# The down projection of a SwiGLU feed-forward in seven block products, with the weight differences made during the input projection

## The chip, the cores and the metric

One NeuronCore of a Trainium2 chip runs the whole program; the other seven are idle. The metric is the device time of one execution in microseconds. Engine names are those of the profile: PE multiplies matrices, DVE, ACT and POOL work element by element, SP issues transfers.

## The reference, cut to what matters

One decoder layer over 2048 prompt rows and 8 x 4 sample rows, d_model 1024, feed-forward width 2816. The part that changes is the last product of the feed-forward:

```python
def _swiglu(x, g, w_gate, w_up, w_down):
    h = _rmsnorm(x, g)
    return (jax.nn.silu(h @ w_gate) * (h @ w_up)) @ w_down

x = x + jnp.concatenate([att, u * gate], axis=-1) @ w_out
x = x + _swiglu(x, norm2_g, w_gate, w_up, w_down)      # then a last RMSNorm
```

The outputs are float32, and the products are made on PE from operands that are split into a high and a low part, as (high, high), (high, low) and (low, high): each product of two blocks is three matmuls.

## The kernel before, in words

The program runs in three stretches: the input projection (its last matmul starts at 565 us; the sample rows' attention stands between its products), the prompt's attention (to about 884 us), and then output projection and feed-forward in three blocks of token tiles of 128 rows: tiles 0-5, 6-11, and 12-15 with the sample rows. All matmuls stand on PE in an order written by hand; a clock of steps (`tick`, `later`, and in the input projection `Plan.at`) puts the other engines' work between them. Each engine, SP included, takes its instructions in the order in which they were written.

In a block the feed-forward goes over 22 chunks of 128 hidden columns. For a chunk f, `product` makes seven block products q = 0..6 of gate and up projection together (lines L1607 to L1609, twelve matmuls of 384 columns each, 272 in the last block). That part is already a scheme of seven products in place of eight. Its seven weight operands per chunk are made from sources that lie in `ab_d` (block 0 makes them and stores them; the others load them), by `high` on ACT (L1546) and `low_half` on POOL (L1550). Each product's result goes to one of four PSUM banks (`ps_m`) and is added up by DVE (L1619 to L1636); `hidden` multiplies silu(gate) by up (L1653), splits the result into `hw`, high on ACT (L1657) and low on DVE (the row of L1275 or L1642).

The down projection is plain. Every two chunks, at q = 3, 4 and 5 of an even chunk, `down_unit` takes one token tile after the other: for each half of the 1024 output columns six matmuls of 512 columns (two chunks by three parts, L1680) go to one of two banks `ps_o`, and DVE adds the bank to the tile's accumulator `acc` (L1682). Two weight rows of 128 x 1024 (`load_down`, one buffer `fd`) are split by ACT (L135) and POOL (L138) for it.

Between two blocks, `next_block` runs the last pair's down products (`first_downs`, L1696 and L1698, then `down_unit`), and in the same time splits the next block's inputs (`split_cat`, L1365 on ACT and L1366 on DVE) and output weights (`split_wo`), finishes the old tiles (`final_a`, `final_b` L1716, `final_store` L1722) and loads the new ones (`load_acc` L1303). Then come the output projection's first half for all tiles (`open_unit`), its second half (`second_unit`), and the norm.

In the input projection POOL has the products of the sample rows' keys (L536), the gate's layer norm (L383) and low halves (L138); PE waits for the low halves `vnl` in the gate products at L412.

## Time and profile before

| what | value |
|---|---|
| runs | 2497.45, 2494.05, 2496.11 us; median 2496.11 us |
| profiled execution | span 2494.2 us, 39114 instructions; the page gives no other time for it, and the span lies 1.9 us under the median of the runs |
| PE, weight load, DVE, ACT, POOL busy | 98%, 85%, 51%, 45%, 52% of the span |
| granted PE clock, mean | 0.990 |
| down matmuls (L1680 and L1696) | 2112 of 128 rows and 88 of 64 rows, all 512 columns wide |
| bytes moved | 455.36 MB, mean 183 GB/s |

Busy times are unions over an engine's instructions. Matmuls overlap in the records, so the mean length of one is not the distance from one to the next; that distance is read from a run of them.

### The profile page before, as it was taken

Reading aid. Unit: us, or ns where it says so; the run is one execution under the profiler, and the core shown is the slowest. Engines: PE = TensorE matmul, PEld = TensorE weight load, DVE = VectorE, ACT = ScalarE, POOL = GpSimd, SP = SyncE. Lnnn points to the kernel's source line nnn. Section 1 sums busy time; section 2 is a strip of 40 time slices with the busy share of each in tenths; the row PEclk is TensorE's granted clock in tenths of the full one; section 3 lists DMA queues with packets and bytes.
Section 4 is the critical chain, followed back from the end, with each engine's and each line's share of the span. In section 5 each row is a group of like instructions: output and inputs, shape, how many; then the busy total and the mean of one; then the engine's idle time right before and its main releaser. Section 6 shows DMA issues by size and latency. Waiting matters only on the chain.

```text
span 2494.2 us, 39114 instructions
## 1 busy us (share of the span) xinstructions
PE 2434.1 (98%) x14022; PEld 2114.0 (85%) x14022; DVE 1265.1 (51%) x2595; ACT 1131.2 (45%) x2449; POOL 1300.3 (52%) x1019
## 2 busy tenths in 40 slices
PE   9999999999999999999999999999999999999997
PEld 7877776667888678999999988999999987999997
DVE  4557573216767644444444465444444466444445
ACT  6324343226667556555455356323323345444334
POOL 2216441004777636777677544544545534676665
PEclk9999999999999899999999999999999999999999
DMA  9874835685555463646556372553544554665553
GB/s 297 274 232 150 271 110 160 201 268 184 173 177 160 117 215 114 195 152 193 167 160 195 126 228 101 192 189 132 196 179 151 203 163 140 224 210 187 189 194 136
DMA packets 292292, 455.36 MB, mean 183 GB/s; under 512 B 28711, under 2 KB 160984, under 8 KB 286980
## 3 DMA queue, kind: packets, MB, share of 16 engines
q1 hardware_dynamic: 285252, 440.82, 54.1%
q10 hardware_dynamic: 6848, 12.06, 1.7%
q8 instruction: 111, 1.82, 0.3%
q14 instruction: 81, 0.66, 0.1%
HBM read 365.07 MB, written 157.84 MB: 210 GB/s over the span
## 4 chain that ended last, share of the span: by engine, by line
PE 73%; DVE 2%; POOL 2%; ACT 2%; issue 1%; DMA 1%; SPq 0%; DVEq 0%; ACTq 0%; POOLq 0%
PE ps_o L1680 19%; PE ps_m L1609 11%; PE ps_m L1607 11%; PE ps_m L1608 11%; PE ps_s L856 2%; PE ps_o L911 2%; PE ps_t L883 1%; PE ps_s L935 1%; PE ps_s L318 1%; PE ps_o L1374 1%; PE ps_o L1376 1%; PE ps_o L1375 1%; PE ps_m L1374 1%; PE ps_s L320 1%; PE ps_s L319 1%
## 5 line engine op out<-in xcount | busy, mean ns | idle before, releaser
L1550 POOL TENSOR_TENSOR op<-fr,op 128x512 fp32r<-128x512 f32 x385 | 487.3, 1296 | 259.3 <-ACT op L1546 245.2
L1607 PE MATMUL ps_m<-xh,op 128*128 128x384 f32 (+3 forms) x1904 | 604.9, 318 | 0.9 <-ACT xh L1451 0.5
L1609 PE MATMUL ps_m<-xh,op 128*128 128x384 f32 (+3 forms) x1904 | 604.6, 318 | 0.0
L1608 PE MATMUL ps_m<-xl,op 128*128 128x384 f32 (+3 forms) x1904 | 603.9, 317 | 0.1
L1680 PE MATMUL ps_o<-dw,hw 128*128 128x512 f32 x2040 | 480.5, 391 | 4.0 <-DVE acc L1682 3.3
L1680 PEld LDWEIGHTS ps_o<-dw,hw 128*128 128x128 f32 x2040 | 380.4, 188 | 82.5 <-DVE acc L1682 5.1
L1607 PEld LDWEIGHTS ps_m<-xh,op 128*128 128x128 f32 x1904 | 360.4, 189 | 5.3 <-ACT xh L1451 0.7
L1608 PEld LDWEIGHTS ps_m<-xl,op 128*128 128x128 f32 x1904 | 360.0, 189 | 4.0 <-DVE xl L1463 0.4
L1682 DVE TENSOR_TENSOR acc<-acc,ps_o 128x512 f32<-128x512 f32 (+1 forms) x362 | 248.1, 687 | 224.8 <-PE ps_o L1680 224.8
L1609 PEld LDWEIGHTS ps_m<-xh,op 128*128 128x128 f32 x1904 | 359.9, 189 | 0.0
L1647 ACT ACTIVATE ps_t<-zn 128x384 f32<-128x384 f32 (+1 forms) x126 | 58.3, 463 | 469.3 <-DVE zn L1630 381.5
L1546 ACT ACTIVATE op<-fr 128x512 fp32r<-128x512 f32 x396 | 235.4, 624 | 25.6 <-DMA fr<-ab_d 21.0
L138 POOL TENSOR_TENSOR dw<-fd,dw 128x1024 fp32r<-128x1024 f32 x66 | 158.6, 2403 | 162.9 <-ACT dw L135 162.9
L318 PE MATMUL ps_s<-wh,xh 128*128 128x512 f32 x480 | 197.5, 411 | 6.1 <-ACT xh L135 6.1
L320 PE MATMUL ps_s<-wh,xl 128*128 128x512 f32 x480 | 189.6, 395 | 0.0
L319 PE MATMUL ps_s<-wl,xh 128*128 128x512 f32 x480 | 189.5, 395 | 0.0
L1550 POOL TENSOR_TENSOR op<-pair,op 128x512 fp32r<-128x512 f32 x63 | 81.3, 1298 | 113.6 <-ACT op L1546 109.2
L536 POOL TENSOR_TENSOR pr<-kv,qb 96x512 f32<-96x512 f32 x32 | 44.3, 1383 | 172.4 <-DMA kv<-in_cache_k_dram 90.8
L318 PEld LDWEIGHTS ps_s<-wh,xh 128*128 128x128 f32 x480 | 91.5, 191 | 48.8 <-issue 23.7
L1657 ACT ACTIVATE hw<-ps_t 128x384 fp32r<-128x384 f32 (+1 forms) x126 | 54.7, 450 | 162.0 <-DVE ps_t L1653 162.0
L927 POOL CAST sq<-k 128x512 fp32r<-128x512 f32 x32 | 34.0, 1063 | 164.1 <-PE ps_s L319 164.1
L1518 ACT ACTIVATE fr<-fr,g2c 128x128 f32<-128x128 f32 x352 | 108.3, 388 | 0.0
(490 smaller groups left out, 4277.0 us busy)
## 6 DMA issues: line engine op xcount, KB each, us to landing
fr<-ab_d SPq DMA_DIRECT2D x308, 256.0 KB
fd<-in_w_down_dram SPq DMA_DIRECT2D x66, 512.0 KB
out_ks_dram<-in_cache_k_dram SPq DMA_DIRECT2D x56, 512.0 KB
out_vs_dram<-in_cache_v_dram SPq DMA_DIRECT2D x56, 512.0 KB
ab_d<-fr SPq DMA_DIRECT2D x88, 256.0 KB
qk_d<-pair SPq DMA_DIRECT2D x64, 256.0 KB
ab_d<-pair SPq DMA_DIRECT2D x63, 256.0 KB
kv<-in_cache_k_dram SPq DMA_DIRECT2D x64, 192.0 KB
```

Of the source, the lines that this page charges most:

```text
L138: (eng_lo or pool).tensor_sub(lo, src, hi.bitcast(F32))
L318: pe.matmul(o[j], xh[:, k, :], wh, start=(k == 0), stop=False)
L319: pe.matmul(o[j], xh[:, k, :], wl, start=False, stop=False)
L320: pe.matmul(o[j], xl[:, k, :], wh, start=False, stop=(k == KD - 1))
L1518: act.activation(w_[:, k * P:(k + 1) * P], w_[:, k * P:(k + 1) * P], AF.Copy, scale=g2c[:, kk:kk + 1])
L1546: act.activation(ops[f, j][0], ab[f][j], AF.Copy)
L1550: (pool if f or j in POOL_LOW else dve).tensor_sub(lo_, ab[f][j], hi.bitcast(F32))
L1607: pe.matmul(out, wh[:, ks], xh[:, :, k], start=(k == 0), stop=False)
L1608: pe.matmul(out, wh[:, ks], xl[:, :, k], start=False, stop=False)
L1609: pe.matmul(out, wl[:, ks], xh[:, :, k], start=False, stop=(k == 3))
L1680: pe.matmul(ps[0:nr], l_, r_[:, cs], start=(z == 0 and y == 0), stop=(z == FC - 1 and y == len(pairs) - 1))
L1682: dve.tensor_add(B.acc[i][0:nr, cs], B.acc[i][0:nr, cs], ps[0:nr])
```

## The change: what it does

The down projection's operands are cut in a 2 x 2 scheme: the two rows of blocks are the two token tiles of a pair, the shared dimension is the two chunks of a pair (f = 2n, 2n + 1), the columns are the two halves of the 1024. Seven block products replace the eight, with sums and differences on both sides (`TO` says to which accumulator each is added, `FRESH` which ones start a bank anew; the others go on adding in the same bank after DVE has read it).

- Weights: `down_rows`, `down_sums` and `down_keep` run at steps 80 to 210 of the input projection. For each of 11 pairs they load two 128 x 1024 rows, make four sums of 128 x 512 on POOL and store the seven 128 x 512 sources in a new array `dd_d`. In the feed-forward `load_dw` fetches one source per product into one of two places, issued right after the product that used the place before; `split_dw`, two steps ahead of the product, splits it by ACT and by POOL (odd products of the first and last block: DVE).
- Hidden values: an even chunk's values are kept in `h0`; `h_even` and `h_odd` make four sums per pair on DVE and split seven operands (`hop`) by ACT and DVE, in place of four splits.
- Products: `down_product` runs one of the seven every second step, for all pairs of tiles; each one's results are added to `acc` by DVE right away. The gate and up products keep three banks in place of four.
- Between blocks, `next_block` runs the product left over from the pair before and the last pair's seven, with `h_odd` between them. The old tiles are finished from step 9 on, one per step (before: from step 2 on, every second step); the new tiles' first additions come 4 steps later, their half-1 weights 2 steps later.
- The very last pair of the last block stays plain (`plain_down`).

On DVE between block 0 and block 1 (`acc`: accumulators, `ps_o`, `ps_m`: banks of the down products, `ps_t`, `h`: hidden values, `zn`, `raw`: sums, `hop`, `hw`: operands, `xl`: the next block's inputs), before:

```order
L1653 TENSOR_TENSOR ps_t0_14560<-ps_t0_14560,raw_14541 128x384
L1642 TENSOR_TENSOR hw_14646<-ps_t1_14621,hw_14646 128x6x64
L1642 TENSOR_TENSOR hw_14646<-ps_t0_14560,hw_14646 128x6x64
L1698 TENSOR_TENSOR acc0_9112<-acc0_9112,ps_o2_14670 128x512
L1698 TENSOR_TENSOR acc0_9112<-acc0_9112,ps_m2_14671 128x512
L1698 TENSOR_TENSOR acc1_9110<-acc1_9110,ps_o3_14672 128x512
L1698 TENSOR_TENSOR acc1_9110<-acc1_9110,ps_m3_14673 128x512
L1366 TENSOR_TENSOR xl2_14658<-xl2_14658,xh2_14657 128x1024
```

and in the changed kernel:

```order
L1797 TENSOR_TENSOR ps_t0_14976<-ps_t0_14976,raw_14941 128x384
L1645 TENSOR_TENSOR op_15063<-op_15063 128x512
L1712 TENSOR_TENSOR zn_15117<-h0_9266,ps_t0_14976 128x3x64
L1712 TENSOR_TENSOR zn_15117<-h0_9266,ps_t1_15057 128x3x64
L1713 TENSOR_TENSOR zn_15118<-zn_15117,h0_9266 128x384
L1662 TENSOR_TENSOR acc0_9289<-acc0_9289,ps_o2_15067 128x512
L1662 TENSOR_TENSOR acc2_9543<-acc2_9543,ps_o3_15072 128x512
L1662 TENSOR_TENSOR acc4_9639<-acc4_9639,ps_m3_15077 128x512
L1682 TENSOR_TENSOR hop_10053<-zn_15118,hop_10053 128x384
L1721 TENSOR_TENSOR raw_15144<-ps_t0_14976,zn_15118 128x3x64
L1682 TENSOR_TENSOR hop_10054<-ps_t0_14976,hop_10054 128x3x64
L1721 TENSOR_TENSOR raw_15144<-ps_t1_15057,zn_15118 128x3x64
```

Two operand rows and then one addition for every six matmuls have become sums and splits that stand between the additions, and one addition for every three matmuls: 24 of them up to the first row of the output projection, where there were 12.

On POOL in the first half's gate columns (`vnl`, `zn`: the gate's low halves and layer norm, `pr`: key products), before:

```order
L138 TENSOR_TENSOR vnl<-zn,vnh 128x512
L536 TENSOR_TENSOR pr<-kv,qb 96x512
L536 TENSOR_TENSOR pr<-kn,qb 128x512
L383 TENSOR_TENSOR zn<-zn,lnb 128x512
L138 TENSOR_TENSOR vnl<-zn,vnh 128x512
L383 TENSOR_TENSOR zn<-zn,lnb 128x512
L536 TENSOR_TENSOR pr<-kv,qb 96x512
```

and in the changed kernel (`tw`, `tu`: rows and sums of the down weights):

```order
L385 TENSOR_TENSOR zn<-zn,lnb 128x512
L140 TENSOR_TENSOR vnl<-zn,vnh 128x512
L632 TENSOR_TENSOR tu<-tw 128x512
L629 TENSOR_TENSOR tw<-tw 128x512
L385 TENSOR_TENSOR zn<-zn,lnb 128x512
L632 TENSOR_TENSOR tu<-tw 128x512
L632 TENSOR_TENSOR tu<-tw,tu 128x512
L538 TENSOR_TENSOR pr<-kv,qb 96x512
```

The four sums of a pair stand between two layer-norm rows and ahead of the key products.

The diff, cut to its core:

```diff
@@ ps_m
-            turn[3] = which = (turn[3] + 1) % 4
+            turn[3] = which = (turn[3] + 1) % 3
@@ new: weight sums
+    def down_rows(n):
+        for z in range(2):
+            dn[n, z] = w_ = sp.tile([P, 2, DA], F32, name="tw", tag="tw", bufs=2)
+            f = 2 * n + z
+            sync.dma_start(w_, A["w_down"][f * P:(f + 1) * P, :].rearrange("p (a c) -> p a c", a=2))
+    def down_sums(n, j):
+        (b11, b12), (b21, b22) = ((dn[n, z][:, 0], dn[n, z][:, 1]) for z in range(2))
+        if j == 1:
+            pool.tensor_sub(b12, b12, b11)
+            return
+        dn[n, "t", j] = t_ = sp.tile([P, DA], F32, name="tu", tag="tu", bufs=3)
+        pool.tensor_sub(t_, *((b22, b12) if j == 3 else (b22, b12) if j == 2 else (b21, dn[n, "t", 2])))
@@ plan of the input projection
+    for n, s0 in enumerate([80, 89, 98] + [134 + 10 * i for i in range(NF // 2 - 3)]):
+        at(s0, "misc", down_rows, n)
+        for j, x in ((3, 3), (1, 3), (2, 4), (4, 4)):
+            at(s0 + x, "out", down_sums, n, j)
+        for j, x in ((3, 5), (0, 5), (2, 6), (4, 6), (1, 6)):
+            at(s0 + x, "store", down_keep, n, j)
@@ new: products
+    PLACE = (0, 4, 5, 6, 2, 1, 3)
+    TO = ((0, 0), (0, 1), (1, 1), (1, 0), (0, 0), (1, 1), (0, 1))
+    FRESH = (0, 4, 5)
+    SLOT = (2, 4, 6, 8, 10, 12, 14)
+    def load_dw(B, k, place=None):
+        n, p = divmod(k, 7)
+        B.dw[k] = x = place or B.ring[k % 2]
+        sync.dma_start(x[1].bitcast(F32), dd_d[n, :, PLACE[p]])
+    def split_dw(B, k):
+        hi, lo_ = B.dw[k]
+        act.activation(hi, lo_.bitcast(F32), AF.Copy)
+        (dve if k % 2 and (B.last or B.b0 == 0) else pool).tensor_sub(lo_, lo_.bitcast(F32), hi.bitcast(F32))
+    def down_product(B, k):
+        n, p = divmod(k, 7)
+        ...
+        for j in range(B.nt // 2):
+            if new:
+                B.chain[j] = bank(2 + j) if j < 2 else ps_m(3)
+            ps, ts = B.chain[j], slice(j * P, (j + 1) * P)
+            for y, (l_, r_) in enumerate(((hh[:, ts], dh), (hh[:, ts], dl), (hl[:, ts], dh))):
+                pe.matmul(ps, l_, r_, start=(new and y == 0), stop=(y == 2), skip_group_check=True)
+            x = B.acc[2 * j + odd]
+            dve.tensor_add(x[:, cs], x[:, cs], ps)
+        ...
@@ new: operands of an odd chunk (a11, a21 from h0; a12, a22 from this chunk)
+    def h_odd(B, u, part):
+        ...
+        if part == 0:
+            ...
+            for z in range(2):
+                dve.tensor_add(u["s1"][:, :, z], a21[:, :, z], a22[z])
+            dve.tensor_sub(u["s2"], u["s1"], a11)
+            high_of(B, 1, u["s2"], 0, n)
+            for z in range(2):
+                high_of(B, 3, a22[z], 0, n, z)
+        elif part == 1:
+            lows_of(B, 1, u["s2"], 0, n)
+            u["s4"] = op_view(raw_tile()[:, 0:n * P], 0, n)
+            for z in range(2):
+                dve.tensor_sub(u["s4"][:, :, z], a12[z], u["s2"][:, :, z])
+                lows_of(B, 3, a22[z], 0, n, z)
+                high_of(B, 4, a12[z], 0, n, z)
+            high_of(B, 5, u["s1"], 0, n)
+        else:
+            for z in range(2):
+                lows_of(B, 4, a12[z], 0, n, z)
+            high_of(B, 6, u["s4"], 0, n)
+            lows_of(B, 5, u["s1"], 0, n)
+            lows_of(B, 6, u["s4"], 0, n)
@@ hidden
-        dve.tensor_mul(g, g, c)
-        ...
-        act.activation(hi, g[:, :, 0:64], AF.Copy)
-        lows = [(lo_, g[:, :, 0:64], hi.bitcast(F32))]
+        if f % 2:
+            dve.tensor_mul(g, g, c)
+            ...
+        else:
+            h = B.h0[:, :, a // 2:b // 2, zz].rearrange("p o j w -> p j o w")
+            dve.tensor_mul(h, *(x.rearrange("p (j o w) -> p j o w", o=2, w=B.w) for x in (g, c)))
@@ next_block
-            later(2 + 2 * y, fn)
+            later(9 + y, fn)
         for y, i in enumerate(order):
-            later(12 + 2 * y, first_end, B, i)
+            later(16 + 2 * y, first_end, B, i)
-        for fn in downs:
-            fn()
+        K = 7 * (NF // 2 - 1)
+        for y in range(-1, 7):
+            if 0 <= y + 1 < 3:
+                h_odd(prev, prev.u, y + 1)
+            if y == -1:
+                split_dw(prev, K + 6)
+            down_product(prev, K + y)
+            split_wo(B, 0, y + 1, lambda s: op_tile())
+            tick()
@@ steps of a block
+            for n in (f // 2 - 2, f // 2 - 1, f // 2):
+                for p in range(7):
+                    k, t_ = 7 * n + p, 14 * (n + 1) + SLOT[p]
+                    ...
+                    if x == t_ - 2:
+                        split_dw(B, k)
+                    if x == t_:
+                        down_product(B, k)
+                    t_ = 14 * ((k - 2) // 7 + 1) + SLOT[(k - 2) % 7] if k > 1 else 9 + k
+                    if x == t_:
+                        load_dw(B, k)
```

More of the change, by code (lines that the diff above doesn't have):

```diff
@@ new lines, in load_dw @@
+    def load_dw(B, k, place=None):
[8 more added lines that the diff above has]
+        n, p = divmod(k, 7)
+        dh, dl = B.dw.pop(k)
+        hh, hl = B.hop[p]
+        odd, half = TO[p]
+        cs = slice(half * 512, (half + 1) * 512)
+        new = p in FRESH
+        for j in range(B.nt // 2):
[6 more added lines that the diff above has]
+            dve.tensor_add(x[:, cs], x[:, cs], ps)
+        if B.last and p in (0, 4, 5, 6):
+            if p < 6:
+                B.chain["s"] = ps_m(3)
+            ps = B.chain["s"][0:2 * SR]
+            hs_ = hs4[:, n % 2 * 2 + (p in (4, 6))]
+            for y, r_ in enumerate((dh, dl)):
+                pe.matmul(ps, hs_, r_, start=(p < 6 and y == 0), stop=(y == 1), skip_group_check=True)
+            x = B.acc[B.nt]
+            for half in ((0, 1), (0,), (), (1,))[(0, 4, 5, 6).index(p)]:
+                cs = slice(half * 512, (half + 1) * 512)
+                dve.tensor_add(x[0:2 * SR, cs], x[0:2 * SR, cs], ps)
@@ new lines, in op_view, with lows_of, high_of, h_even @@
+    def op_view(x, a, b):
+        return x.rearrange("p (j z c) -> p j z c", z=2, c=64)[:, a:b]
+    def lows_of(B, p, src, a, b, z=None):
+        hi, lo_ = (op_view(x, a, b) for x in B.hop[p])
+        if z is not None:
+            hi, lo_ = hi[:, :, z], lo_[:, :, z]
+        dve.tensor_sub(lo_, src, hi.bitcast(F32))
+    def high_of(B, p, src, a, b, z=None):
+        hi = op_view(B.hop[p][0], a, b)
+        act.activation(hi if z is None else hi[:, :, z], src, AF.Copy)
+    def h_even(B, u):
+        a, b = u["a"] // 2, u["b"] // 2
+        a11, a21 = (B.h0[:, o, a:b, :, 0:64] for o in range(2))
+        plain = B.last and u["f"] + 2 == NF
+        high_of(B, 0, a11, a, b)
+        if plain:
+            s3 = a21
+        else:
+            s3 = op_view(zn_tile()[:, 0:(b - a) * P], 0, b - a)
+            dve.tensor_sub(s3, a11, a21)
+        high_of(B, 2, s3, a, b)
+        lows_of(B, 0, a11, a, b)
+        lows_of(B, 2, s3, a, b)
@@ L1693, in first_downs @@
                 cs = slice(half * 512, (half + 1) * 512)
[L1694 to L1696 removed]
+                plain_down(B, i, half, z, ps, z == 0, z == 1)
                 if z:
@@ L1784, in last_rows @@
         rms_b(c, SR)
-        down_unit(B, 3, pair)
+        down_unit(B, 3)
         rms_c(b, P)
```

174 lines of the change are left out of this document (98 added, 76 removed).

## The prediction

> **What bounds the kernel now.** I read the page's parts 1 and 4 first, then the chain of waits in order of time inside block 0, then the stages.
>
> ```profile
> span 2494.2 us, 39114 instructions
> PE 2434.1 (98%) x14022; PEld 2114.0 (85%) x14022; DVE 1265.1 (51%) x2595; ACT 1131.2 (45%) x2449; POOL 1300.3 (52%) x1019
> PE ps_o L1680 19%; PE ps_m L1609 11%; PE ps_m L1607 11%; PE ps_m L1608 11%; PE ps_s L856 2%; PE ps_o L911 2%; PE ps_t L883 1%; PE ps_s L935 1%; PE ps_s L318 1%; PE ps_o L1374 1%; PE ps_o L1376 1%; PE ps_o L1375 1%; PE ps_m L1374 1%; PE ps_s L320 1%; PE ps_s L319 1%
> ...
> 1043.24 5.48 PE ps_o L1680 x24
> 1050.83 5.48 PE ps_o L1680 x24
> ...
> 1088.88 5.48 PE ps_o L1680 x24
> ```
>
> The longest single line of the chain is the down projection, L1680. A tile pair's 24 matmuls take 5.48 us, 0.228 us each; the same place of the next pair of chunks comes 45.64 us later (1088.88 - 1043.24). The rest of those 45.64 us, 29.2 after three such tile pairs, is fourteen gate and up products of twelve matmuls, 2.09 us each. So here every matmul that is left out counts, as long as the others keep up. Whether they do is a question by stage (columns: us, then busy PE, PEld, DVE, ACT, POOL, granted clock, DMA share, GB/s):
>
> ```profile
> 187.00:250.00 63.00, 57.39 (x263) 45.88 (x262) 50.40 (x118) 27.79 (x50) 41.10 (x31) 0.96 0.50 150
> 306.00:470.00 164.00, 159.59 (x781) 118.16 (x779) 82.06 (x159) 58.14 (x99) 40.20 (x30) 1.00 0.50 156
> 1020.00:1445.00 425.00, 425.00 (x2244) 398.63 (x2243) 187.69 (x317) 212.41 (x519) 300.80 (x221) 1.00 0.52 166
> 1445.00:1460.00 15.00, 13.55 (x58) 10.31 (x58) 11.68 (x21) 9.23 (x15) 7.42 (x5) 1.00 0.98 275
> 1530.00:1945.00 415.00, 414.62 (x2260) 390.04 (x2259) 187.53 (x335) 141.14 (x265) 211.39 (x153) 1.00 0.49 170
> 2025.00:2045.00 20.00, 18.80 (x84) 14.76 (x83) 14.94 (x29) 10.86 (x19) 7.42 (x5) 1.00 0.80 244
> 2130.00:2470.00 340.00, 340.00 (x2241) 313.35 (x2241) 165.76 (x365) 132.33 (x300) 220.75 (x158) 1.00 0.57 197
> ```
>
> Inside the blocks (rows 3, 5 and 7) PE has no gap, and DVE has half of its time left. The gaps are at the boundaries (rows 4 and 6) and in the input projection (rows 1 and 2).
>
> **The matmuls removed.** A block of six tiles had 6 x 2 x 22 x 3 = 792 down matmuls of full height; now 11 pairs x 7 products x 3 tile pairs x 3 = 693. The last block had 528; now 10 x 7 x 2 x 3 = 420, and 48 for its plain last pair. That is 99 + 99 + 60 = 258 fewer; the sample rows keep their 88. 258 x 0.228 = **-58.9 us**.
>
> **Inside a block.** These rows price what DVE, ACT and POOL get:
>
> ```profile
> L1682 DVE TENSOR_TENSOR acc<-acc,ps_o 128x512 f32<-128x512 f32 x340 | 233.3, 688 | 217.8 <-PE ps_o L1680 217.8
> L1275 DVE TENSOR_TENSOR hw<-ps_t,hw 128x384 fp32r<-128x384 f32 x80 | 42.6, 553 | 50.9 <-ACT hw L1657 48.8
> L1275 DVE TENSOR_TENSOR hw<-ps_t,hw 128x256 fp32r<-128x256 f32 x40 | 16.8, 420 | 2.4
> L1550 DVE TENSOR_TENSOR op<-fr,op 128x512 fp32r<-128x512 f32 x11 | 9.7, 884 | 3.7 <-ACT op L1546 1.9 <-POOL woh L138 1.8
> L1550 POOL TENSOR_TENSOR op<-fr,op 128x512 fp32r<-128x512 f32 x385 | 487.3, 1296 | 259.3 <-ACT op L1546 245.2
> L1546 ACT ACTIVATE op<-fr 128x512 fp32r<-128x512 f32 x396 | 235.4, 624 | 25.6 <-DMA fr<-ab_d 21.0
> L138 POOL TENSOR_TENSOR dw<-fd,dw 128x1024 fp32r<-128x1024 f32 x66 | 158.6, 2403 | 162.9 <-ACT dw L135 162.9
> ```
>
> Per pair of chunks in block 0, DVE gets 21 bank additions for 12 (+9 x 0.688 = 6.2), three more low halves (1.7), four sums of 384 (2.2), 0.6 for eight that are cut in two, and half of the weights' low halves (3.5 x 0.884 = 3.1): 13.8 us on top of 20.2 (187.69 x 45.64 / 425), 34.0 of the 43.6 us that a pair then has, 78%. In the last block (pair: 33.9 us, from the two transfer rows below) it is 16.6 before, plus eight additions (5.5), 1.3, 1.7, 0.6 and 3.1: 28.8 of 32.6, 88%. That is under PE's time, but in bursts: at q = 0 to 2 of an even chunk the sums, a down product's additions and the sample's come to 10.9 us against 8.2 of PE. DVE is then 2.7 us late, which two steps of PE (3.0 us) take up before the next product writes those banks. POOL splits 7 x 1.30 (or half of that) where it had 2 x 2.40, and ACT is busy for 34 to 50% of these stages. I take **+3 us** for all three blocks; the ends are 0 and 8 (0.25 us for each of the 32 pairs).
>
> **The boundaries.** Here DVE has no gate and up products to hide behind:
>
> ```profile
> L1366 DVE TENSOR_TENSOR xl<-xl,xh 128x1024 fp32r<-128x1024 f32 x11 | 13.8, 1258 | 2.4 <-ACT xh L1365 2.4
> ```
>
> PE's eight products there are 72 matmuls, 16.4 us. Each writes the three banks that DVE must have read since the product before, so PE goes at DVE's pace. DVE's list until it lets the last product start: the last chunk's addition and multiplication (1.1), 21 additions (14.4), the twelve instructions of `h_odd` (four of 384 at 0.553, eight of 192 at 0.353, an estimate on the line through 256 and 384: 5.0), two inputs' low halves (2.5). The last product starts with the first of its predecessor's three additions and takes 2.05: 1.1 + 14.4 + 5.0 + 2.5 - 1.4 + 2.1 = 23.7 us, 7.3 over PE's own. At the second boundary one of the inputs comes later: 6.0. PE's old gaps at these places go (15.00 - 13.55 and 20.00 - 18.80 in rows 4 and 6: 2.65). Sum **+10.6**. The lower end is that the lists overlap fully: -2.65.
>
> Queued behind this are the old tiles' finish and the new tiles' loads, in turn on SP:
>
> ```profile
> 1458.04 0.71 SPq L1722 DMA_DIRECT2D out_yp_dram<-acc  x1
> 1465.31 0.33 SPq L1303 DMA_DIRECT2D acc<-in_x_prompt_dram  x1
> ```
>
> A store and the load that waits for it take 7.3 us in that stretch, six tiles of them some 40. The finish now starts about 22 us later and the second half of the output projection about 7 us later, so the sixth tile's input, which DVE must have before it can add the second units' results queued behind, arrives about when it is wanted. **+1**, other end +10.
>
> The clock could make the boundary dearer. It is full where PE has two thirds of 5 us, and halved after it had a quarter:
>
> ```profile
> 200.00:205.00 5.00, 3.46 (x15) 2.52 (x15) 3.67 (x9) 1.40 (x3) 4.69 (x4) 1.00 0.24 70
> 930.00:935.00 5.00, 1.39 (x6) 0.72 (x4) 2.68 (x7) 4.00 (x13) 0.00 (x0) 0.83 0.33 105
> 935.00:940.00 5.00, 4.51 (x13) 3.76 (x14) 2.96 (x10) 3.98 (x11) 2.97 (x3) 0.50 0.14 52
> ```
>
> At the boundary PE would have 16.4 of 23.7, 69%, like the first of these rows, so I charge nothing. The Trainium skill, "TensorE: Matmul & The Clock Gate", section "A second HAM failure mode: psum-queue depth-cycling", speaks against the change at this point: a kernel that cycled through PSUM banks had short idle times between its groups often enough that the clock went back and forth. By that rule the sum would be the one of the second rival; the first of these rows does not bear it out, and no row here has this pattern for 20 us.
>
> **The input projection.** POOL gets 44 subtractions (1.30 each, 57 us), SP 77 transfers, 11.5 MB read and 20.2 written back at 128 x 512 and 128 x 1024. The first three pairs fall into 187 to 250 us, the other eight into 306 to 470. Nothing there needs the results, but POOL makes the gate's low halves in the same order, and PE waits for those already:
>
> ```profile
> PE ps_t L412 <- POOL vnl L138: 1.3, 1, 1.3
> PE ps_t L412 <- DVE un L420: 2.8, 3, 1.6
> ```
>
> Five bursts of 5.2 us (pairs 1 to 3, 6 and 7) stand in front of gate work. POOL has 41.1 of 63 us in the first stretch, 56.7 with three of them; PE stands idle for 5.6 there now. Between 0 and 5 x 5.2 = 26 I take 2 us each, **+10**: nearer the lower end, since in the second stretch POOL works 40 of 164 us.
>
> **Sum.** 2494.2 - 58.9 + 3 + 10.6 + 1 + 10 = 2459.9 for the span. The span lay 1.9 under the median of the runs shown, so the median becomes **2462 us**, 34 less, 1.4%. With all low ends but the boundary's it is 2448, with the middle of the high ones 2478.
>
> **Rivals.**
>
> First, the boundaries are hidden (12%): DVE's sums slip between the additions, and PE loses nothing there. For: a product starts bank by bank. Against: DVE's list is longer than PE's. Time: 2462 - 10.6 - 2.65 - 10 for gate bursts that find POOL free = 2439.
>
> Second, the clock halves at the boundaries (8%): 72 matmuls at 0.456 are 32.8 us in place of 23.7, twice: 2462 + 18 = 2480. For: the gaps come every 2 us; against: the row at 200.
>
> Third, the transfers of the input projection fill the DMA engines (12%). The two stretches run at share 0.50 with 150 and 156 GB/s, so 300 to 312 is all there is; 8.65 MB in 63 us and 23.1 in 164 add 137 and 141: 96% and 95%. If only 275 GB/s can be had, as in the row at 1445, the work runs over by 3 and 13 us: w_in rows and cached values come late, and 2462 + 16 = 2478. Against: weights are fetched nine steps ahead.
>
> Fourth, slower (9%): the two places for weights limit the down products. A place is loaded after its product, split, and used again four steps later.
>
> ```profile
> 2259.83 0.33 SPq L1589 DMA_DIRECT2D fd<-in_w_down_dram  x1
> ...
> 2293.77 0.33 SPq L1589 DMA_DIRECT2D fd<-in_w_down_dram  x1
> 2297.33 1.06 ACT L135 ACTIVATE dw<-fd 128x1024 fp32r<-128x1024 f32 x1 [2.43 <-DMA fd<-in_w_down_dram]
> ```
>
> From issue to use twice the bytes took 3.56 us; with 0.62, 1.30 and a product of 1.6 the round is 7.1 us, and four steps of the last block are 9.3 (four gate and up products of 1.51, which is a fourteenth of 33.94 less 56 x 0.228, and two of 1.6), of the others 12.4. It decides from 9.3 on: each us above costs 35 us in the last block, and above 12.4 70 more in the others. At 11.5, a load of 8 us as by the slow store above, the time is 2462 + 77 = 2539. Against it: the 3.56 us were measured at the last block's DMA share.
>
> **Chances and range.** Forecast 55%, rivals 12, 8, 12 and 9; 4% for mixtures that end near the time before. The forecast's own range is 2448 to 2478. Eight in ten needs the second and third rival and part of the first: 2440 to 2488. A measurement of this kernel tells 0.2%, 5 us, from no change: faster 86%, same 4%, slower 10%.
>
> **What would show it.** In the changed profile: L1660 with 1806 rows at 0.228 us in groups of nine inside the blocks, and a pair of chunks in 43.6 us; at the boundaries PE waiting on DVE's `acc` for 6 to 8 us each; in 187 to 250 us 3 to 8 us more of PE idle time, before L412; no wait of PE on `hop` splits. A pair above 45 us, or waits on `hop` or `dd_d`, would make the prediction wrong in the blocks; a boundary without waits, or one at half clock, in its second term.

## The result and the profile after

The changed kernel takes 2558.21 us (median, 2548.64 to 2561.07), the kernel before 2495.08 on the same chip: a ratio of 1.025, 95% interval 1.0228 to 1.0272. It is slower by 63 us where the prediction had it faster by 34. The profiled execution has a span of 2557.5 us against 2494.2. One of the four executions of run 3 below took 6006 us, so that run's time is that of the other three.

The stages below are cut at the first and the last gate or up product of each block, so that "boundary" holds the eight down products that are left over, the output projection and norm2 of the next block.

| stage, us | before | after | difference | forecast |
|---|---|---|---|---|
| up to the first gate/up product | 950.4 | 980.0 | +29.6 | +10 |
| block 0 | 495.3 | 499.7 | +4.4 | -21.6 |
| first boundary | 88.2 | 95.6 | +7.4 | +5.9 |
| block 1 | 492.2 | 474.4 | -17.8 | -21.6 |
| second boundary | 78.7 | 94.1 | +15.4 | +4.7 |
| block 2 | 363.9 | 385.3 | +21.4 | -14.5 |
| end | 25.5 | 28.4 | +2.9 | +2.8 |

(The forecast's column is its own terms put to their stages: 99, 99 and 68 matmuls fewer at 0.228 us and 1 us a block for "inside a block"; the end has 8 matmuls more, and the 1 us for late accumulators is put there.)

The page's part 1 and two of its costliest groups:

```profile
span 2557.5 us, 40544 instructions
PE 2421.8 (95%) x13764; PEld 2080.4 (81%) x13764; DVE 1710.7 (67%) x3302; ACT 1242.6 (49%) x2773; POOL 1441.3 (56%) x1152
L1645 POOL TENSOR_TENSOR hop<-hop 128x512 fp32r<-128x512 f32 x140 | 186.5, 1332 | 173.9 <-ACT hop L1644 158.6
L1644 ACT ACTIVATE hop<-hop 128x512 fp32r<-128x512 f32 x210 | 130.9, 623 | 56.6 <-DMA hop<-dd_d 54.7
```

258 matmuls are gone, and PE is busy for only 12 us less, with 76 us more of idle time. The same stretches by stage as before (columns as in the prediction):

```profile
187.00:250.00 63.00, 51.24 (x214) 39.86 (x213) 47.68 (x104) 23.58 (x43) 45.70 (x34) 0.91 0.68 226
306.00:470.00 164.00, 149.75 (x709) 111.60 (x708) 87.29 (x160) 54.80 (x92) 82.77 (x59) 0.96 0.77 248
1040.00:1440.00 400.00, 387.72 (x2010) 359.03 (x2009) 316.38 (x496) 230.29 (x585) 299.19 (x223) 0.99 0.60 186
1620.00:2030.00 410.00, 410.00 (x2160) 384.23 (x2159) 295.44 (x505) 162.32 (x334) 258.30 (x199) 1.00 0.62 198
2160.00:2520.00 360.00, 339.26 (x2174) 303.58 (x2174) 293.12 (x579) 169.45 (x401) 233.27 (x176) 0.99 0.65 210
```

Block 1 (fourth row) has no gap and makes most of its gain. Blocks 0 and 2 and the input projection have gaps, and a granted clock below one. What PE waited for (total, times, longest):

```profile
PE ps_o L1660 <- POOL hop L1645: 26.5, 30, 3.2
PE ps_t L414 <- ACT vnh L137: 12.7, 2, 9.8
PE ps_o L1660 <- DVE acc L1662: 12.6, 9, 2.2
PE ps_t L414 <- DVE un L422: 7.9, 3, 4.0
PE ps_o L1660 <- ACT hop L1644: 6.7, 9, 1.0
```

The first and the last are the down products' weights: the wait that the prediction said must not show (3.9 us more are waits for the halves that DVE makes). The third is the boundaries, as forecast. The other two are the input projection's gate.

**Block 0: POOL's queue.** The chip's order on POOL around one of the stalls, with ACT's high half of the same weights and PE's wait:

```profile
1087.33 1.30 POOL L1583 TENSOR_TENSOR op<-pair,op 128x512 fp32r<-128x512 f32 x1 [2.58 <-ACT op L1579]
1088.59 1.30 POOL L1563 TENSOR_TENSOR pair<-fr 128x512 f32<-128x512 f32 x1
1089.97 1.28 POOL L1566 TENSOR_TENSOR fr<-fr 128x512 f32<-128x512 f32 x1
1091.21 1.61 POOL L1583 TENSOR_TENSOR op<-pair,op 128x512 fp32r<-128x512 f32 x1
1092.78 1.29 POOL L1569 TENSOR_TENSOR pair<-fr 128x512 f32<-128x512 f32 x1
1094.02 1.59 POOL L1645 TENSOR_TENSOR hop<-hop 128x512 fp32r<-128x512 f32 x1
```

```profile
1087.68 0.62 ACT L1644 ACTIVATE hop<-hop 128x512 fp32r<-128x512 f32 x1
```

```profile
1095.66 1.73 PE L1660 MATMUL ps_o<-hop 128*128 128x512 f32 x5 [1.98 <-POOL hop L1645]
```

The high half is there at 1088.3. The low half starts 5.7 us later, since five instructions for the gate and up weights stand ahead of it. It was not the load: ACT had split it already. The pattern comes back every two pairs of chunks (1188.8, 1280.4 and 1373.6 us).

**What a stall costs beyond itself.** The granted clock (third number from the end) around the same stall, in slices of 1 us (in so short a slice the DMA figures count whole transfers that start in it):

```profile
1094.00:1095.00 1.00, 0.00 (x0) 0.00 (x0) 1.00 (x2) 0.90 (x2) 1.00 (x2) 1.00 1.56 589
1097.00:1098.00 1.00, 1.00 (x3) 0.76 (x3) 0.69 (x2) 0.00 (x0) 1.00 (x2) 0.50 0.00 0
1098.00:1099.00 1.00, 1.00 (x4) 0.86 (x3) 0.41 (x2) 0.00 (x0) 1.00 (x2) 0.50 0.00 0
1100.00:1101.00 1.00, 1.00 (x7) 1.00 (x7) 0.20 (x1) 0.00 (x0) 0.00 (x0) 1.00 0.90 347
```

After 2 us without a matmul the clock is half for 3.4 us (1096.6 to 1100.0), which is 1.7 us more. Idle time of PE and time lost to half a clock, from the same trace: 17.7 and 6.8 us in block 0, 1.9 and 0 in block 1, 20.9 and 7.2 in block 2. Before they were 1.7 and 1.7, 0.4 and 0, 0.1 and 3.1.

**The input projection: POOL's burst, then a chain.** One pair's subtractions (L632, L629) on POOL (at the dots stand a low half of the gate, L140, and the third subtraction), the layer norm's addition behind them (L385), ACT's split behind that, and PE's wait:

```profile
372.45 1.29 POOL L385 TENSOR_TENSOR zn<-zn,lnb 128x512 f32<-128x512 f32 x1
373.70 1.30 POOL L632 TENSOR_TENSOR tu<-tw 128x512 f32<-128x512 f32 x1
375.08 1.48 POOL L629 TENSOR_TENSOR tw<-tw 128x512 f32<-128x512 f32 x1
...
379.13 1.29 POOL L632 TENSOR_TENSOR tu<-tw,tu 128x512 f32<-128x512 f32 x1
380.37 1.26 POOL L385 TENSOR_TENSOR zn<-zn,lnb 128x512 f32<-128x512 f32 x1
```

```profile
381.67 0.63 ACT L137 ACTIVATE vnh<-zn 128x512 fp32r<-128x512 f32 x1 [6.30 <-POOL zn L385]
```

```profile
390.22 0.58 PE L414 MATMUL ps_t<-vnh,wg_h 128*128 128x256 f32 x1 [9.82 <-ACT vnh L137]
```

With the four subtractions, 5.4 us, in POOL's queue, PE stands idle for 9.8 us. ACT waited 6.3 us in its queue, and behind it stood the scaling (L336) for which DVE's layer norm of the next tile waited, and that one went through POOL and ACT again. Not all of the 9.8 us is the subtractions': runs 2 and 8 below take the stall apart.

### The profile page after: what moved, and what is told of

Read it like the earlier page. It is cut to its first block, busy times and chain, and to the rows that moved or that the text cites. A ratio compares the mean times of both kernels' runs of the same rounds, so it can differ in the third digit from the quotient of the medians.

```text
span 2557.5 us, 40544 instructions
## 1 busy us (share of the span) xinstructions
PE 2421.8 (95%) x13764; PEld 2080.4 (81%) x13764; DVE 1710.7 (67%) x3302; ACT 1242.6 (49%) x2773; POOL 1441.3 (56%) x1152
## 5 line engine op out<-in xcount | busy, mean ns | idle before, releaser
L1583 POOL TENSOR_TENSOR op<-fr,op 128x512 fp32r<-128x512 f32 x385 | 511.6, 1342 | 221.3 <-ACT op L1579 116.8
L1660 PE MATMUL ps_o<-hop 128*128 128x512 f32 x1260 | 343.4, 403 | 37.3 <-POOL hop L1645 26.5
L1662 DVE TENSOR_TENSOR acc<-acc,ps_o 128x512 f32<-128x512 f32 x448 | 295.2, 682 | 26.9 <-PE ps_o L1660 20.6
L1660 PEld LDWEIGHTS ps_o<-hop 128*128 128x128 f32 x1260 | 230.6, 189 | 90.4 <-POOL hop L1645 38.7
L1645 POOL TENSOR_TENSOR hop<-hop 128x512 fp32r<-128x512 f32 x140 | 186.5, 1332 | 173.9 <-ACT hop L1644 158.6
L1644 ACT ACTIVATE hop<-hop 128x512 fp32r<-128x512 f32 x210 | 130.9, 623 | 56.6 <-DMA hop<-dd_d 54.7
L320 PEld LDWEIGHTS ps_s<-wh,xh 128*128 128x128 f32 x480 | 92.0, 192 | 49.2 <-issue 23.7
L1660 PE MATMUL ps_m<-hop 128*128 128x512 f32 x420 | 121.2, 397 | 0.0
L1583 POOL TENSOR_TENSOR op<-pair,op 128x512 fp32r<-128x512 f32 x63 | 86.9, 1382 | 50.9 <-ACT op L1579 50.8
L322 PEld LDWEIGHTS ps_s<-wh,xl 128*128 128x128 f32 x480 | 92.0, 192 | 20.8 <-DVE xl L140 0.2
```

The lines of the kernel that those rows point to most:

```text
L320: pe.matmul(o[j], xh[:, k, :], wh, start=(k == 0), stop=False)
L322: pe.matmul(o[j], xl[:, k, :], wh, start=False, stop=(k == KD - 1))
L1583: (pool if f or j in POOL_LOW else dve).tensor_sub(lo_, ab[f][j], hi.bitcast(F32))
L1644: act.activation(hi, lo_.bitcast(F32), AF.Copy)
L1645: (dve if k % 2 and (B.last or B.b0 == 0) else pool).tensor_sub(lo_, lo_.bitcast(F32), hi.bitcast(F32))
L1660: pe.matmul(ps, l_, r_, start=(new and y == 0), stop=(y == 2), skip_group_check=True)
```

## Experiments

Ten kernels were run. Stage times are cut as in the table above, from each run's one profile; "last input matmul" is the end of the input projection's last matmul, 566.0 us before and 596.4 after. How far such times scatter is seen where a run leaves a stage as it is: the last input matmul ends at 596.0, 602.4, 598.3 and 601.7 us in runs 3, 4, 5 and 7, and block 2 takes 381.7, 384.2 and 384.6 us in runs 1, 2 and 8 (385.3 in the changed kernel). Where they are left as they are, blocks 0 and 1 repeat within 2 us.

**1. Ten of the eleven pairs left out of the input projection.**

```diff
-    for n, s0 in enumerate([80, 89, 98] + [134 + 10 * i for i in range(NF // 2 - 3)]):
+    for n, s0 in enumerate([112]):
...
-        sync.dma_start(x[1].bitcast(F32), dd_d[n, :, PLACE[p]])
+        sync.dma_start(x[1].bitcast(F32), dd_d[0, :, PLACE[p]])
```

> Left out: the sums, loads and stores of ten of the eleven pairs of chunks in the input projection (one pair is kept, moved to 250 us); all down products then multiply with that pair's weights. The feed-forward has the same instructions. The input projection's last matmul stood at 565.1 us before and at 595.5 after the change. Both theories on this stage (POOL's bursts of subtractions; the transfers) expect the 30 us back: last matmul at 566 to 570, time 2528 to 2534, blocks 0, 1 and 2 unchanged at 500, 474 and 385 us. If the blocks become shorter, the loss there hung on the input projection, which no theory says.

2531.93 us, ratio 1.015 [1.0131, 1.017]. The last input matmul came at 572.2, since the one pair that was kept cost some 4.5 us where it was put (250 to 306 us). Block 0 took 499.5, block 1 474.4, block 2 381.7 us. So the blocks lose their time by themselves; the input projection's loss is the pairs' own.

**2. The transfers without the subtractions.**

```diff
-        for j, x in ((3, 3), (1, 3), (2, 4), (4, 4)):
-            at(s0 + x, "out", down_sums, n, j)
...
-            sync.dma_start(dd_d[n, :, j + 2], dn.pop((n, "t", j)))
+            sync.dma_start(dd_d[n, :, j + 2], dn[n, 1][:, j % 2])
```

> Left out: the 44 subtractions of w_down on POOL; every load and every store stays (in place of a difference, a block of the rows is stored). Theory A (POOL's bursts stand in front of the layer norm's additions and the gate's low halves, and the clock falls after each stall): last matmul of the input projection at 566 to 572, time 2529 to 2535. Theory B, the prediction's third rival (the transfers fill the DMA engines): 585 or later, time 2548 to 2558.

2541.88 us, 1.0187 [1.0171, 1.0204]; last input matmul at 580.6. Neither theory had that: 14.6 us of the 30.4 are the transfers' alone, 15.8 go with the subtractions. The DMA share was 0.79 and 0.82 in the two stretches. PE waited 4.3 us for cached values (`pr<-in_cache_v_dram`, 0.2 before) and 3.3 us for the gate's high halves (none before).

**3. The halves of the down weights first in their step, in all blocks.**

```diff
+            for n in (f // 2 - 2, f // 2 - 1, f // 2):
+                for p in range(7):
+                    if 0 <= n < NF // 2 - 1 and 7 * f + q == 14 * (n + 1) + SLOT[p] - 2:
+                        split_dw(B, 7 * n + p)
             if f and q < 2:
                 prepare(B, f, 7 + q)
...
-                    if x == t_ - 2:
-                        split_dw(B, k)
```

> The two halves of a block of down weights are issued at the start of their step, ahead of that step's work on the gate and up weights, in all three blocks; nothing else moves. Theory C (in block 0 the low half stands in POOL's queue behind two to four instructions of 1.3 us for the gate and up weights): block 0 goes from 499.7 us to 476 to 482, with PE's waits for POOL's hop at L1645 there down from 16 us to below 3; block 2 (385 us) shorter by 0 to 8; time 2530 to 2540. Theory D, the prediction's fourth rival (the load into one of two places comes late): no change beyond 3 us, 2555 to 2560.

2716.98 us, 1.089 [1.0863, 1.0916]. Theory C was right on block 0 (481.7 us, waits for POOL's halves 16.0 down to 4.0), and nothing had foreseen the rest: block 1 went from 474 to 573 us and block 2 from 385 to 460. SP and ACT in block 1 of this run:

```profile
1722.21 0.38 SPq L1640 DMA_DIRECT2D hop<-dd_d  x1
...
1730.02 5.50 SPq L1538 DMA_DIRECT2D fr<-ab_d  x2
...
1736.39 0.53 SPq L1640 DMA_DIRECT2D hop<-dd_d  x1
```

```profile
1725.17 0.63 ACT L1644 ACTIVATE hop<-hop 128x512 fp32r<-128x512 f32 x1 [4.57 <-DMA hop<-dd_d]
```

ACT now stands at the split until the load has landed (295 us in all in block 1, 11 in the changed kernel), with the gate weights' high halves behind it in its queue, and POOL's low halves after those. They free the `fr` buffers for which SP waits at L1538 (5.5 us), and the next load of down weights stands behind that on SP. The round closes, and a product comes every 6.3 to 10.3 us, 7.5 in the middle, instead of every 6.27. In block 2 the low halves on DVE wait likewise, and the bank additions stand behind them (63 us of waits for `acc`). Late loads are what the prediction's fourth rival feared, but not by its two places: in block 1 SP waits 358 us for the `fr` buffers and 13 for a place. The round is read from this trace; no run opens it in block 1 alone.

**4. Four places for down weights in block 2.**

```diff
+        w = n if B.last else 384
         for p in range(7):
-            x = ts[p // 2][:, p % 2 * 768:]
-            B.hop.append((x[:, 0:n], x[:, 384:384 + n]))
+            x = ts[p // 2][:, p % 2 * 2 * w:]
+            B.hop.append((x[:, 0:n], x[:, w:w + n]))
...
+        if B.last:
+            B.ring = [(x[:, 1024:1536], x[:, 1536:]) for x in ts]
```

> Block 2 alone: its hidden values need 256 columns where 384 were kept, and the columns set free hold four places for down weights in place of two, so each load is issued four products ahead, not two. When a block is split is unchanged. Theory D (late loads): block 2 goes from 385 us to 352 to 362, time 2526 to 2536. Theory E (in block 2 the splits are late because ACT and DVE reach them late, DVE's subtractions in SBUF taking 1.2 to 1.5 us while POOL works, 0.4 to 0.7 alone): only the stalls in which ACT waited for a DMA go, about a quarter; block 2 at 373 to 382, time 2547 to 2555. Blocks 0 and 1 as they were.

2557.34 us, 1.0243 [1.0223, 1.0263]; block 2 381.8 us, 3.5 less, which is no more than its scatter. Theory D is out, and the block is where theory E had it: in the changed kernel late loads are at most a small part.

**5. Each block its own order.** Block 0 as in run 3, block 1 as it was, block 2 with the four places and the halves two products ahead.

```diff
-                    if x == t_ - 2:
+                    if x == t_ - (4 if B.last else 2) and B.b0:
```

> Block 0 issues the two halves at the start of their step (as in the run before last), block 1 does as in the changed kernel, block 2 has the four places and issues the halves two products ahead of use, not one. Theory C and E together (what was late are the halves, behind other work in the queues of POOL, ACT and DVE, not the loads): block 0 at 480 to 484 us (499.7 in the changed kernel), block 1 at 474, block 2 at 351 to 362 (385.3), time 2510 to 2522. Theory D (PE then waits for the loads instead): block 2 at 375 or more. Theory F, DVE is simply full in block 2: waits of PE on hop are replaced by waits on DVE's acc at L1662 as in the run with the halves first, block 2 at 380 or more.

2519.78 us, 1.0099 [1.0082, 1.0115]. Block 0 481.6, block 1 474.5, block 2 360.6 us; no wait for `hop` is left in block 2, and waits for DVE (`acc`, `raw`) of 8.3 us came up. C and E stand: the halves were late in the queues of POOL, ACT and DVE. 43 us of the blocks' loss are back. In block 2 places and order changed together; run 4 has the places alone.

**6. The pairs moved away from the gate work; all low halves of block 2 on POOL.** On the kernel of run 5; a pair's four subtractions also stand in four steps in place of two.

```diff
-    for n, s0 in enumerate([80, 89, 98] + [134 + 10 * i for i in range(NF // 2 - 3)]):
+    for n, s0 in enumerate([50, 64, 108, 118, 128, 138, 174, 187, 200, 213, 226]):
...
-        (dve if k % 2 and (B.last or B.b0 == 0) else pool).tensor_sub(lo_, lo_.bitcast(F32), hi.bitcast(F32))
+        (dve if k % 2 and B.b0 == 0 else pool).tensor_sub(lo_, lo_.bitcast(F32), hi.bitcast(F32))
```

> The run with the halves placed by block, and two things more. In the input projection the pairs of chunks are moved out of the two stretches of gate work (187 to 250 and 356 to 403 us) to where POOL was idle (403 to 566 us) or nearly so, and the four subtractions stand in four steps in place of two. In block 2 all low halves are on POOL. If theory A is right and the transfers cost what they did in the run without subtractions only where they lie in the gate stretches: last matmul of the input projection at 568 to 578 us (596 in the changed kernel, 581 without subtractions), time 2480 to 2500. If the transfers cost the same wherever they lie: 580 or later. Block 2: DVE relieved of 35 subtractions of 0.7 to 1.4 us: if DVE's lateness was what held it, shorter than in the other run by 2 to 8 us; if POOL's queue holds it, longer.

2526.75 us, 1.0121 [1.0106, 1.0137]. Block 2 gained (356.4 us, 4.2 less than in run 5: DVE's lateness had still cost something), and the input projection got worse than with any other version: 613.0 us. A stretch into which pairs were moved, in this run and then in the kernel before:

```profile
306.00:356.00 50.00, 38.36 (x144) 29.03 (x144) 28.32 (x39) 16.32 (x24) 29.41 (x20) 0.84 0.92 303
```

```profile
306.00:356.00 50.00, 50.00 (x225) 41.37 (x224) 39.31 (x65) 18.46 (x31) 22.71 (x18) 1.00 0.44 140
```

At a DMA share of 0.92, PE is idle for 11.6 of 50 us. POOL's queue in that stretch shows one way in which late transfers reach PE, here for 3.3 us:

```profile
312.90 1.29 POOL L632 TENSOR_TENSOR tu<-tw 128x512 f32<-128x512 f32 x1 [14.97 <-DMA kv<-in_cache_k_dram]
...
315.37 2.34 POOL L140 TENSOR_TENSOR xl<-xr,xh 128x1024 fp32r<-128x1024 f32 x1
```

```profile
317.76 0.79 PE L322 MATMUL ps_s<-wh,xl 128*128 128x512 f32 x1 [3.29 <-POOL xl L140]
```

POOL stands for 15.0 us at a subtraction whose operands have not landed, and an input's low half, for which PE waits, stands behind it. So the third rival's late transfers exist, with the denser packing. Taking the pairs out of the gate work did not help where it put them beside other transfers.

**7. POOL quiet in block 2.**

```diff
+        if turn[-1] == "last":
+            act.activation(lo_, ab[f][j], AF.Copy)
+            return
         (pool if f or j in POOL_LOW else dve).tensor_sub(lo_, ab[f][j], hi.bitcast(F32))
```

> Left out, in block 2 of the changed kernel: POOL's low halves of the gate and up weights, for which ACT copies the weight (the products are wrong from there on); so POOL has only every second low half of the down weights in that block. If DVE's subtractions with all operands in SBUF are slowed by POOL working at the same time: DVE's L1682 on 128x256 in block 2 falls from a mean of 0.93 us to 0.41 to 0.55, L1645 on DVE from 1.05 to 0.70, and L1662, which reads PSUM, stays at 0.68. If their time depends on something else (the layout, the strides), they stay. ACT gets 0.6 us per low half more, so PE's waits may go either way; the block's time is no test here.

One run. DVE's instructions in block 2 by shape, in the changed kernel and then here (count, busy us, mean ns; the line numbers are seven higher there):

```profile
L1662 DVE TENSOR_TENSOR acc<-acc,ps_o 128x512 f32<-128x512 f32 x134 | 87.9, 681 | 8.6 <-PE ps_o L1660 7.9
L1645 DVE TENSOR_TENSOR hop<-hop 128x512 fp32r<-128x512 f32 x34 | 35.0, 1028 | 8.1 <-ACT hop L1644 7.6
L1682 DVE TENSOR_TENSOR hop<-raw,hop 128x256 fp32r<-128x256 f32 x10 | 14.3, 1433 | 2.0 <-ACT hop L1686 2.0
L1682 DVE TENSOR_TENSOR hop<-ps_t,hop 128x128 fp32r<-128x128 f32 x40 | 10.3, 276 | 0.3 <-ACT hop L1686 0.3
```

```profile
L1669 DVE TENSOR_TENSOR acc<-acc,ps_o 128x512 f32<-128x512 f32 x138 | 91.2, 683 | 8.2 <-PE ps_o L1667 7.9
L1652 DVE TENSOR_TENSOR hop<-hop 128x512 fp32r<-128x512 f32 x35 | 24.2, 691 | 14.0 <-ACT hop L1651 13.7
L1689 DVE TENSOR_TENSOR hop<-raw,hop 128x256 fp32r<-128x256 f32 x10 | 4.3, 425 | 7.5 <-ACT hop L1693 7.5
L1689 DVE TENSOR_TENSOR hop<-ps_t,hop 128x128 fp32r<-128x128 f32 x40 | 10.3, 276 | 0.8 <-ACT hop L1693 0.8
```

With POOL quiet, the subtractions whose operands all lie in SBUF take 0.69 and 0.43 us instead of 1.03 and 1.43. Those that read a PSUM bank take the same in both. Block 2 took 365.8 us here, but POOL's queue is emptied as well, so that this time does not tell what the durations alone cost.

**8. The subtractions without the transfers.** Pairs 1 to 10 use pair 0's tiles.

```diff
+            if n:
+                dn[n, z] = dn[0, z]
+                continue
             dn[n, z] = w_ = sp.tile([P, 2, DA], F32, name="tw", tag="tw", bufs=2)
...
     def down_keep(n, j):
+        if n:
+            return
```

> Left out: the loads and stores of w_down rows for pairs 1 to 10 in the input projection; all 44 subtractions stay where they are, on the rows of pair 0, and the down products all use pair 0's weights. With the run without subtractions this splits the input projection's 30.4 us (last matmul 566.0 before, 596.4 changed, 580.6 with transfers alone). If the two prices add: 15.8 for POOL, last matmul at 579 to 585, time 2540 to 2546. If the stalls come only from both together: 570 or less. Here POOL never waits for a load, so its bursts can only start earlier.

2544.36 us, 1.0201 [1.0186, 1.0217]; last input matmul at 584.9, 18.9 late with pair 0's transfers in it. With run 2's 14.6 that is 33.5, inside the 30.0 to 36.4 of the kernels that have both: the two prices add. The subtractions' came from the pairs in the two stretches of gate work (14.3 us by 305 us, 18.2 by 398 us); those after it cost 0.7, and there the transfers did. Matmul by matmul, the work that PE did at 356 to 395 us before, with the stall of 9.8 us in it, cost 11.8 us in the changed kernel, 5.3 in run 2 and 4.8 here.

**9. Eight pairs in attention.** On the kernel of run 6, three pairs at 310 to 370 us, eight in attention.

```diff
+    for i, n in enumerate(range(len([134, 144, 154]), NF // 2)):
+        s0 = 246 + 18 * i
+        at(s0, "misc", late_rows, n)
+        at(s0 + 5, "store", late_plain, n)
+        at(s0 + 8, "store", late_sum, n, 0, 1, 0)
...
+        at(s0 + 14, "store", late_keep, n, (3, 4), (2, 6))
```

> The kernel with the halves placed by block (all low halves of block 2 on POOL), and eight of the eleven pairs of chunks are loaded, subtracted and stored during attention, one pair every 18 of its 160 steps, in one tile of 8 KB per partition; three stay at 310 to 370 us of the input projection, where the transfers alone cost nothing. Attention ran at a DMA share of 0.54 (165 GB/s; the pairs add 23 MB in 290 us, 79 GB/s) with POOL at 203 of 290 us (42 us more). If a transfer costs only where the DMA engines are near full and a subtraction only where a chain waits for POOL: last matmul of the input projection at 566 to 571, attention 289.5 to 296 us long (290 in the changed kernel), blocks 481, 474 and 356, time 2483 to 2496, the same as before or a little faster. If POOL sets attention's pace with them: attention at 305 or more, time 2500 or more.

2510.35 us, 1.0073 [1.006, 1.0085]; last input matmul at 577.4. PE lost nothing under the first two of the three early pairs and 10.3 us under the third, at the burst shown above at 373.7 us; run 10 shows that this was not the third's alone. From the last input matmul to the output projection it is 315 us, 294 in the changed kernel, as the expectation's second reading had it: PE waits 11.4 us for DVE's `st` there (3.2 in the changed kernel) and 7.9 us for POOL (1.9). That stretch in the changed kernel and then here, with POOL at 243 us and the DMA share at 0.71:

```profile
596.00:890.00 294.00, 286.22 (x2587) 236.62 (x2586) 205.91 (x526) 203.62 (x526) 204.07 (x219) 0.98 0.54 166
```

```profile
577.00:892.00 315.00, 290.13 (x2588) 238.42 (x2588) 215.10 (x526) 205.89 (x526) 243.02 (x251) 0.98 0.71 228
```

**10. The pairs at the places that were cheapest**: two at 310 to 350 us, five at 400 to 510, four in attention.

```diff
-    for n, s0 in enumerate([134, 144, 154]):
+    for n, s0 in enumerate([134, 144, 174, 184, 194, 204, 214]):
...
-        s0 = 246 + 18 * i
+        s0 = 250 + 36 * i
```

> The last kernel with the pairs of chunks at the places that were cheapest so far: two at 310 to 350 us of the input projection (nothing in the last run), five at 400 to 510 us (in the changed kernel four pairs there came to 8 us, all of it the transfers' by the run with the subtractions alone), four in attention, one every 36 steps (eight came to 20 us). If each pair keeps its price where it lies: last matmul of the input projection at 574 to 579 us, attention 299 to 302 us long, blocks 481, 474 and 356, time 2495 to 2503, still slower than before. If the prices hang on how dense the pairs lie in attention: attention at 292 to 297, time 2488 to 2496.

2501.14 us, 1.0023 [1.0014, 1.0033]: 57 us less than the changed kernel and still a quarter of a per cent more than before. Attention took 298.3 us: at half the density a pair costs about 1 us there instead of 2.6. The input projection ended at 584.7, 6 us over the range. A wait of 5.9 us at L414 stands in the gate work at 375 us though no pair lies there; in all PE loses 6.7 us there. The trace leads it back to the pair before, whose subtractions hold POOL from 343.0 to 348.7 us, ahead of key products:

```profile
350.02 0.68 DVE L543 TENSOR_REDUCE S_s<-pr 96x8 f32<-96x512 f32 x1 [3.09 <-POOL pr L538]
355.33 0.20 ACT L376 ACTIVATE ln_r<-ln_v 128x1 f32<-128x1 f32 x1 [9.45 <-DVE ln_v L371]
358.77 1.30 POOL L385 TENSOR_TENSOR zn<-zn,lnb 128x512 f32<-128x512 f32 x1 [5.05 <-ACT zn L384]
```

DVE waits for a key product, the layer norm's statistics stand behind that, ACT waits for those, and the layer norm's first addition on POOL comes at 358.8 us (350.1 before). So the second pair was not free: its price shows one stretch later. This is a reading of one trace; no run leaves that pair out. No version beat the kernel before.

## Why the prediction was wrong

**The matmuls removed (-58.9)** were right in number, not in time. Without idle time and half a clock, blocks 0, 1 and 2 are 16.7, 19.3 and 3.4 us shorter, where the counts give 22.6, 22.6 and 15.5. In groups of nine or six with three or two places to write the down matmuls take 0.231 us each instead of 0.228, and the gate and up products between them 0.5% more: some 9 us of the 21 that are missing. In block 2 another 6.8 came back in run 5; the rest is open.

**"Inside a block I take +3 us; the ends are 0 and 8."** This is the step that failed. Idle time and half a clock come to 54 us in the three blocks, 7 before: 47 us in place of 3. It rests on two errors. Runs 3 and 5 show the first; run 7 shows the second, but not what it cost.

One was to add up what POOL, ACT and DVE get and to compare it with PE's time. These totals were about right: DVE is busy for 316 of 400 us in block 0 and 293 of 360 in block 2, 79% and 81%, forecast 78% and 88%, and POOL's total in block 0 is nearly what it was (299 of 400 us; before 301 of 425). The halves are late all the same: they were put behind other work of the same step, while a product wants them two steps later. The prediction looked for lists in order at the boundaries and not here. Run 3 took 18 us off block 0 by the order alone, and earlier halves with four places took 25 off block 2 in run 5.

The other was the durations. The low halves and sums were costed at 0.55 us, from rows that read PSUM (`hw<-ps_t`), the weights' low halves at 0.88. The chunks' values now lie in SBUF in `h0` and `raw`, and a subtraction with both inputs in SBUF takes 1.0 to 1.4 us beside POOL. The prediction's own rows hinted at it: `op<-fr,op` on DVE at 884 ns, against 688 for `acc<-acc,ps_o`, both 128x512. The Trainium skill, "SBUF — State Buffer", section "Who interferes with whom", says that a VectorE instruction with two SBUF inputs contends with a GpSimd one that reads SBUF, and that, outside its two-port modes, one with at most one SBUF input does not. Run 7 agrees with both halves: 1433 ns down to 425 for the first kind, 276 both times for the second. The prediction had not weighed it.

**The boundaries (+10.6)** were right in kind: PE at DVE's pace, waits for `acc` of 6.5 and 6.0 us. The eight products took 25.5 and 25.2 us, forecast 23.7 and 22.4.

**Late accumulators (+1, end +10)**: mis-sized. Each product writes all pairs of tiles, so no tile is done before the last product, and the new tiles' inputs come in a row after it. At the second boundary the chain reads:

```profile
2104.53 0.63 ACT L1439 ACTIVATE zn<-acc 128x512 f32<-128x512 f32 x1 [4.25 <-DVE acc L1418]
2105.16 1.13 ACT L137 ACTIVATE wol<-fr 128x512 fp32r<-128x512 f32 x2
```

```profile
2105.82 0.44 PE L1412 MATMUL ps_o<-wol,cats 128*64 128x512 f32 x1 [2.51 <-ACT wol L137]
```

The weights' split stands behind a square that waits for the late accumulator: 4.0 us of idle PE in three waits, and a granted clock of 0.74 and 0.69 in the 12 us around them. In the whole second boundary half a clock cost 6.5 us, 0.3 before.

**The input projection (+10, between 0 and 26)**: 30.4, beyond the upper end. In 187 to 250 us PE's idle time rose by 6.2 us, inside the 3 to 8 that the prediction named as a sign; the rest was not in it. It took the transfers as free, and alone they cost 14.6 (run 2). It took a burst as a delay of one engine, 2 us each, 10 in all; the layer norm goes through ACT, DVE and POOL and back for each tile, and the subtractions cost 16 to 19 us (runs 2 and 8).

**The rivals.** The third (transfers fill the DMA engines, +16) came about beside the forecast's own term: 14.6, at shares of 0.79 and 0.82 where it had 0.95. The second said 2480 for a clock that halves at the boundaries; it halves there in part (0.75 in one stretch of 5 us; 8.2 us lost at both, 0.3 before), but its larger share is inside blocks 0 and 2, 14.0 us, 4.8 before. The rule of the Trainium skill that the prediction set aside there ("TensorE: Matmul & The Clock Gate", section "A second HAM failure mode: psum-queue depth-cycling"), that short idle times between groups of matmuls make the clock go back and forth, the trace bears out in part: in block 2 three pairs of stalls of 0.9 us (at 2174, 2216 and 2506 us) are followed by half a clock, others of that length are not. The fourth came nearest in time (2539) and in place, waits for the weights' halves. That is luck: its mechanism, a load late for want of a place, is not seen beyond the scatter in run 4, and the late loads of run 3, 99 us in block 1, came from SP's queue.

## What to carry to other kernels

That an engine has time left in a stage says nothing of an instruction with a due time: read from the trace what stands ahead of it in its queue, and give what a product waits for its place before the work that has slack. But moving a wait forward puts everything behind it at risk; here the same edit gave one block 18 us and took 99 from the next. Before costing an operation by a row, see that the row reads the same memories and has the same neighbours.

## What was not expected of the hardware

Stalls of the same length, 1.98 us, were followed by half a clock or not: at 1095.7 and 1280.4 us half a clock for 3.41 us came after it, at 1188.8 and 1373.6 us the clock stayed full. The trace has the reason. Every change of the granted clock lies on one grid of 3.41 us (the half-clock stretches at 1028.3, 1096.6 and 1280.9 us begin 20 and 54 of its steps apart). The first two stalls lie whole inside one step of the grid, and the one at 1373.6 us is cut in two by an edge, 1.48 us before it. Counted so from 950 us to the last matmuls, each step at full clock in which PE stood idle for 1.76 us or more was followed by half a clock, with one exception (1.91 us, the stall at 1188.8), and none with 1.68 us or less. The Trainium skill, "TensorE: Matmul & The Clock Gate", section "What's actually happening", has a window of 3.4 us that runs free of the program; the trace agrees with that, by the grid above. DVE's subtraction of 128x256 took 0.43 us with POOL quiet and up to 1.5 beside it, while reading one operand from PSUM made it indifferent to POOL (276 ns for 128x128 either way).
